# Two two-layer transformer blocks on one core: 32 of 48 modulation units as row sums on the vector engine instead of products on TensorE

## The chip, the cores and the metric

The kernel runs on one core of one Trainium2 chip. The metric is the time of one execution on the device in microseconds (us); lower is better. The kernel before takes 1193.03 us (median of three runs, 1192.88 to 1195.18).

## What is computed

Two blocks of two layers each follow one another on 256 tokens of width 1024, all in f32. The first block is attention of several kinds with a gate and a layer norm. The second has a stream of 256 latent tokens and one of 256 context tokens; its layer, cut to what matters here, is

```python
shift_x, scale_x, gate_x = split(silu(c)     @ w_mod + b_mod, 3)   # w_mod: 1024 x 3072
shift_c, scale_c, gate_c = split(silu(c_ctx) @ w_mod + b_mod, 3)
hx = rms_norm(xs, norm_g) * (1 + scale_x) + shift_x                # hc alike
px = hx @ w_in + b_in                                              # 1024 x 7712
ya, yb, yc = conv(px), gla(px), attention(px)                      # three branches
m  = (sigmoid(px[13])*ya + sigmoid(px[14])*yb + sigmoid(px[15])*yc) @ w_out
xs = xs + gate_x * m              # the context stream alike, in the first layer only
```

The **modulation** is the first two lines: two vectors (c and c_ctx) times a 1024 x 3072 matrix, once for each of the two layers. It depends on no token, so it may be computed at any time before its parts are used: shift and scale at the layer's norm, the gate at the layer's end.

## The kernel before

**Weights.** All weights are streamed from DRAM as units of 512 KB (128 partitions x 1024 f32) in one fixed table, by `WStream`. A unit is loaded by SP (L130) into one of `RAW` = 4 raw buffers `wr`; ACT casts it to a high part `wh` (L154); DVE subtracts to get the low part `wl` (L155); both have their own rings of buffers, 5 of `wh` and 5 + `WLX` = 5 of `wl`. The product then takes three matmuls, high by high, high by low and low by high (`mm3`, L184 to L186). `get(key)` is called as a unit's products are written; it first calls `ahead`, which issues the loads up to 6 table entries further on and the splits up to 3 (`LOOK`; 3 and 2 at the start). A scheduler sets the order of the instructions on each engine as the program is built; on the chip each engine works through its own in that order. Unit names in the trace: the first digit is the layer, `0m` the three kinds of merge gates of block two (8 units each), `0oa`, `0gg`, `0og`, `0cg`, `0oc` the branch gates and branch outputs between them, `0o` and `0p` the output product for the two streams, `0AKV`, `0AQ`, `0BQ` the attention's keys, values and queries, `0Va`, `0Vb` the convolution's inputs. Names with a capital letter A to I and `O` are those of block one.

**Modulation.** The 48 units of `w_mod` (2 layers x 3 parts x 8) are not split. They stand in the same table between the others, at the places of `FILL` (a key and a number), and each is taken by `mod_stream` just before the unit of that key: four f32 matmuls of 32 columns of `cz` (silu of c and c_ctx) by 128 x 256 of weights (L770), each recorded as two passes. After the 8 units of a part, ACT copies the sum out of PSUM (`modr`, L775), two small matmuls turn it (`modt`, L778) and DVE adds the bias (L782). The 24 units of layer 0 stand in the second layer of block one (keys 1A to 1H), 16 units of layer 1 in the first layer of block two, and 8 in its second layer.

**The first layer's merges** (about 545 to 820 us) are the longest stretch of one kind: for each of the three branches, eight 512-column merge-gate units and four branch-output units, interleaved, with the GLA branch and the convolution's taps (L1012, one multiply-add of 128 x 512 each) on DVE beside them.

Of the kernel before, what the change touches and what calls it, by code (L numbers as in the profile page):

```python
# [10 lines left out]
F32 = mybir.dt.float32  # L11
# [4 lines left out]
OP = mybir.AluOpType  # L16
# [16 lines left out]
NPA = (2, 3)  # L33
WLX = 0

# [75 lines left out]
class WStream:  # L111
# [118 lines left out]
def block1(g, l, xTh, xTl, xtok, W, last, pre_out=lambda: None, hold=None, each=None):  # L230
# [268 lines left out]
    def fox_gates():  # L499
# [23 lines left out]
        nc.tensor.matmul(ps[:, 128:256], lf[:, 1, :], g.tri, start=True, stop=False)  # L523
        nc.tensor.matmul(ps[:, 128:256], lf[:, 0, :], g.ones, start=False, stop=True)

# [207 lines left out]
def units_mod():  # L733
    return [(f'mod{s}{k}', k, 1, [(D * s, D)]) for s in MORDER for k in range(8)]

# [25 lines left out]

def mod_stream(g, l, W):

    nc, sp, pp = g.nc, g.sp, g.pp
    for s in MORDER:
        ps = pp.tile([128, 256], F32, name=f'mod{l}{s}', tag='gm', bufs=g.GM)
        for k in range(8):
            w = W.whole(f'{l}mod{s}{k}')
            for q in range(4):
                nc.tensor.matmul(ps[32 * q:32 * q + 32], g.cz[:, k // 2, 2 * (k % 2):2 * (k % 2) + 32],  # L770
                                 w[:, 0, 256 * q:256 * q + 256], start=k == 0, stop=k == 7)
            if k < 7:
                yield
        r = sp.tile([128, 256], F32, name=f'modr{l}{s}', tag='tg', bufs=TG)
        nc.scalar.copy(r, ps)  # L775
        pt = pp.tile([128, 2, 4, 2], F32, name=f'modt{l}{s}', tag='at', bufs=g.AT)
        for i in range(2):
            nc.tensor.matmul(pt[:, i].rearrange("p q w -> p (q w)"), r[:, 128 * i:128 * i + 128], g.sel8,  # L778
                             start=True, stop=True)
        ks = slice(8 * s, 8 * s + 8)  # L780
        v = lambda t: t.rearrange("p (q i) w -> p q i w", q=4)
        nc.vector.tensor_add(v(g.mod[l][:, ks, :]), pt.rearrange("p i q w -> p q i w"),  # L782
                             v(g.bmod[l][:, ks, None].to_broadcast([128, 8, 2])))
        if s == 1:

            nc.vector.scalar_tensor_tensor(g.modA[l], g.mod[l][:, ks, :], 1.0,
                                           g.ng[l][:, :, None].to_broadcast([128, 8, 2]), op0=OP.add, op1=OP.mult)
        yield
# [731 lines left out]
def host_arrays(inp):  # L1520
    h = dict(xa=pack_xa(xT_layout(inp['x'][0]), inp['w_in'][0]), xtok=inp['x'][0], ctxt=xT_layout(inp['ctx_2'][0]), cst=consts(CST),
             par1=par1(inp), par2=par2(inp), rowp=rowpar(inp), wup=wup(inp))
    for i, lst in enumerate(CST1):
        h[f'cst1{i}'] = consts(lst)
    for l in range(2):
# [3 lines left out]
        h[f'wm_{l}'] = pack(inp['w_mod_2'][l], units_mod())  # L1529
        h[f'wc_{l}'] = pack(inp['w_conv_out_2'][l], units_out('oc', 4))  # L1530
# [18 lines left out]
def setup(ctx, tc, ins):  # L1549
# [60 lines left out]
def setup_mod(g, ins, W):  # L1610
# [24 lines left out]
def setup2(g, ins):  # L1635
# [7 lines left out]
    for l in L:  # L1643
# [29 lines left out]

# [50 lines left out]
def program(ctx, tc, ins, out, parts=(1, 2)):  # L1724
    g = setup(ctx, tc, ins)
    nc = g.nc
    mods = sum((table(ins[f'wm_{l}'], f'{l}', units_mod()) for l in range(2)), [])
    f32 = {e[0] for e in mods}
    fs = FILL.split()
# [9 lines left out]
    for l in range(2):  # L1739
        t2 = tables2(ins, l)  # L1740
        o = [t2[f'{l}{k}'] for k in order2(l)]
        if l == 0:

            o = o[:7] + [(f'0BQ{i}', *e[1:]) for i, e in enumerate(o[3:7])] + o[7:]
            o += [(f'0p{i}', *e[1:]) for i, e in enumerate(o[-8:])]
        seq += o
    tab, m = [], 0
    for e in seq:
        n = fills.get(e[0], 0)
        tab += mods[m:m + n] + [e]  # L1750
        m += n
# [79 lines left out]
```

## Time and profile before

| | |
|---|---|
| median of three runs | 1193.03 us (1192.88 to 1195.18) |
| profiled execution | 1192.62 us, of which span of the trace 1190.8 us |
| granted TensorE clock | 0.999 |
| PE (TensorE) busy | 1168.5 us, 98% |
| DVE (VectorE) busy | 921.1 us, 77% |
| ACT (ScalarE) busy | 569.5 us, 48% |
| DMA moved | 171.33 MB, mean 144 GB/s |

The span is the traced part of the profiled execution; 1.8 us lie around it. Busy times count an instruction from its start to its end; instructions that follow each other closely on one engine overlap a little, so the distance from one start to the next is what an instruction costs there.

### The profile page before, as it was taken

To read this page: it belongs to the slowest core of one execution; us is meant where nothing else is said; L and a number is where in the kernel's file an instruction comes from. 1 tells how busy PE (TensorE), PEld (TensorE's weight loads), DVE (VectorE), ACT (ScalarE), POOL (GpSimd) and SP (SyncE) were. 2 spreads that over 40 slices of the span, in tenths; PEclk is the share of its full clock that TensorE was granted. 3 is DMA by queue.
4 is the path that set the end of the run, shared out by engine and by line. 5 is a ranking of instruction groups with operands and counts; after the bars stand their busy time and mean duration, and the time that the engine had idled before them with its cause. 6 is when DMAs were issued, how large, how long until landed. Compare 5 with 4: busy or idle time off the path is not lost.

```text
span 1190.8 us, 20632 instructions
## 1 busy us (share of the span) xinstructions
PE 1168.5 (98%) x8024; PEld 975.7 (82%) x8024; DVE 921.1 (77%) x2051; ACT 569.5 (48%) x1024; POOL 11.2 (1%) x42
## 2 busy tenths in 40 slices
PE   8999999999999999999999999999999999999998
PEld 6788777677887777767887888888999778999998
DVE  6996766967799859989545986755799897896984
ACT  5556634456555433247444422433455534855552
POOL 0000000000000000000000000000000000000000
PEclk9999999999999999999999999999999999999999
DMA  7634566465555642024221232325545333554552
GB/s 263 224 125 127 186 207 225 155 229 195 177 194 181 230 137 89 19 73 145 68 84 59 89 100 78 106 89 177 178 142 186 96 107 123 179 162 127 174 176 72
DMA packets 47538, 171.33 MB, mean 144 GB/s; under 512 B 5260, under 2 KB 5900, under 8 KB 46672
## 3 DMA queue, kind: packets, MB, share of 16 engines
q1 hardware_dynamic: 47440, 170.01, 43.7%
q8 instruction: 63, 1.03, 0.3%
q14 instruction: 35, 0.29, 0.1%
HBM read 167.89 MB, written 2.10 MB: 143 GB/s over the span
## 4 chain that ended last, share of the span: by engine, by line
PE 76%; DVE 11%; DMA 6%; ACT 5%; issue 2%; SPq 0%; ACTq 0%; DVEq 0%
PE f0m L186 3%; PE f0m L185 3%; PE f0m L184 3%; PE f1m L186 2%; PE f1m L184 2%; PE f1m L185 2%; PE po L185 1%; PE po L186 1%; PE po L184 1%; PE mod L770 1%; PE go L186 1%; PE go L185 1%; PE go L184 1%; PE yog L186 1%; PE yoc L186 1%
## 5 line engine op out<-in xcount | busy, mean ns | idle before, releaser
L1012 DVE SCALAR_TENSOR_TENSOR ucv<-up,par,ucv 128x512 f32<-128x512 f32 (+1 forms) x240 | 147.3, 614 | 2.8
L184 PE MATMUL f0m<-hTh,wh_0m 128*128 128x512 f32 x192 | 75.1, 391 | 0.0
L185 PE MATMUL f0m<-hTl,wh_0m 128*128 128x512 f32 x192 | 75.1, 391 | 0.0
L186 PE MATMUL f0m<-hTh,wl_0m 128*128 128x512 f32 x192 | 74.8, 390 | 0.0
L184 PE MATMUL f1m<-hTh,wh_1m 128*128 128x256 f32 x192 | 54.9, 286 | 0.1
L186 PE MATMUL f1m<-hTh,wl_1m 128*128 128x256 f32 x192 | 54.8, 286 | 0.0
L185 PE MATMUL f1m<-hTl,wh_1m 128*128 128x256 f32 x192 | 54.5, 284 | 0.0
L154 ACT CAST wh_0m<-wr_0m 128x1024 fp32r<-128x1024 f32 x24 | 25.1, 1047 | 55.9 <-PE f0m L185 14.5
L155 DVE TENSOR_TENSOR wl_0m<-wr_0m,wh_0m 128x1024 fp32r<-128x1024 f32 x24 | 29.3, 1222 | 18.2 <-ACT wh_0m L154 18.1
L184 PEld LDWEIGHTS f0m<-hTh,wh_0m 128*128 128x128 f32 x192 | 36.1, 188 | 7.4
L185 PEld LDWEIGHTS f0m<-hTl,wh_0m 128*128 128x128 f32 x192 | 36.1, 188 | 7.3
L186 PEld LDWEIGHTS f0m<-hTh,wl_0m 128*128 128x128 f32 x192 | 36.1, 188 | 7.3
L184 PEld LDWEIGHTS f1m<-hTh,wh_1m 128*128 128x128 f32 x192 | 36.8, 191 | 0.5 <-ACT wh_1m L154 0.3
L186 PEld LDWEIGHTS f1m<-hTh,wl_1m 128*128 128x128 f32 x192 | 36.7, 191 | 0.2 <-DVE wl_1m L155 0.2
L185 PEld LDWEIGHTS f1m<-hTl,wh_1m 128*128 128x128 f32 x192 | 36.8, 191 | 0.1
L154 ACT CAST wh_1m<-wr_1m 128x1024 fp32r<-128x1024 f32 x24 | 24.9, 1049 | 24.4 <-PE f1m L185 7.6
L155 DVE TENSOR_TENSOR wl_1m<-wr_1m,wh_1m 128x1024 fp32r<-128x1024 f32 x24 | 29.3, 1221 | 8.6 <-ACT wh_1m L154 8.4
L155 DVE TENSOR_TENSOR wl_0o<-wr_0o,wh_0o 128x1024 fp32r<-128x1024 f32 x8 | 9.8, 1224 | 13.2 <-ACT wh_0o L154 13.2
L1413 DVE SCALAR_TENSOR_TENSOR xT<-po,mod,xT 128x256 f32<-128x256 f32 x16 | 7.7, 483 | 14.3 <-PE po L186 14.3
L185 PE MATMUL po<-mgl,wh_0o 128*128 128x256 f32 x64 | 18.2, 285 | 0.0
L186 PE MATMUL pp<-mgh,wl_0p 128*128 128x256 f32 x64 | 18.2, 284 | 0.0
L185 PE MATMUL pp<-mgl,wh_0p 128*128 128x256 f32 x64 | 18.2, 284 | 0.0
(1857 smaller groups left out, 3960.6 us busy)
## 6 DMA issues: line engine op xcount, KB each, us to landing
wr_0mod<-in_wm_dram SPq DMA_DIRECT2D x24, 512.0 KB, 4.5
wr_1mod<-in_wm_dram SPq DMA_DIRECT2D x24, 512.0 KB, 3.7
wr_0m<-in_w_dram SPq DMA_DIRECT2D x24, 512.0 KB, 3.5
wr_1m<-in_w_dram SPq DMA_DIRECT2D x24, 512.0 KB, 3.5
wr_0O<-in_w1o_dram SPq DMA_DIRECT2D x8, 512.0 KB, 3.6
wr_1O<-in_w1o_dram SPq DMA_DIRECT2D x8, 512.0 KB, 3.6
wr_0o<-in_wo_dram SPq DMA_DIRECT2D x8, 512.0 KB, 3.6
wr_0p<-in_wo_dram SPq DMA_DIRECT2D x8, 512.0 KB, 3.7
```

The source lines that it names most:

```text
L154: g.nc.scalar.copy(wh, r)
L155: g.nc.vector.tensor_sub(wl, r, wh.bitcast(F32))
L184: nc.tensor.matmul(out, lh, rh, start=start, stop=False)
L185: nc.tensor.matmul(out, lh, rl, start=False, stop=False)
L186: nc.tensor.matmul(out, ll, rh, start=False, stop=stop)
L770: nc.tensor.matmul(ps[32 * q:32 * q + 32], g.cz[:, k // 2, 2 * (k % 2):2 * (k % 2) + 32], w[:, 0, 256 * q:256 * q + 256], start=k == 0, st ...
L1012: yield nc.vector.scalar_tensor_tensor(o, src, dw[:, i, j:j + 1], o, op0=OP.mult, op1=OP.add)
L1413: nc.vector.scalar_tensor_tensor(r[:, f, :], ps[:, :256], g.mod[l][:, 16 + f, w:w + 1], r[:, f, :], op0=OP.mult, op1=OP.add)
```

## The change

16 units (layer 0, parts 1 and 0) stay as products, at the first seven of the old places, in the second layer of block one. The other 32 units (layer 0 part 2, and all three parts of layer 1) are laid out transposed: a unit holds 256 output columns of `w_mod` on 128 partitions by two, and half (512) of the inner dimension along the row. For each unit DVE does four SCALAR_TENSOR_TENSOR instructions of 128 x 512 that multiply by a broadcast row of silu(c) or silu(c_ctx) (`modc`) and sum along the row with `accum_out`; the product itself goes to a scratch tile `modj` in bf16 that nobody reads. The two halves are added later. The 32 units are spread evenly over the 48 units from `0m3_1` to `0oc3`, the first layer's merges (`DFILL`). `modc` (512 KB, the same 4 KB row on every partition) is loaded by SP twice, once per half, and takes two tanh on ACT and two instructions on DVE each time.

The tiles for this are paid with three others: `wl` has 4 buffers instead of 5 (`WLX`), the table of ones has one column, and the rope table of block two, until now a constant, is loaded by SP twice, once for each layer. `ahead` now counts only split units, so that modulation units in the table no longer shorten the look-ahead.

```diff
-WLX = 0
+WLX = -1
-MORDER = (1, 0, 2)
-FILL = '1B2 2 1E2 3 1D2 3 1F0 2 1G0 2 1H2 1 0Va0 2 0Va1 2 0Va2 2 0GV0 1 0ag0 2 0ag2 2 1GV0 3 1ag0 2 1ag2 2 1A0 1 0BQ2 2 1F2 2 1GK0 1 1B0 1 1A3 5 1C2 1 0ag1 1 1H0 1 0GK0 2'
+FILL = '1A0 1 1A3 5 1B0 1 1B2 2 1E2 3 1C2 1 1D2 3'
+DFILL = ((32, '0m3_1', '0oc3'),)
+LATE = 1
+MODP = [(0, 1), (0, 0)]
+MODD = [(*m, c, h) for ms, hs in (([], (0, 1)), ([(0, 2), (1, 1), (1, 0), (1, 2)], (1, 0)))
+        for h in hs for m in ms for c in range(4)]
...
     def whole(self, key):
         i = self.idx[key]
-        self.ahead(i)
+        while self.nd <= i:
+            self._dma()
...
+    def behind(self, i, n):
+        while n and i < len(self.table) - 1:
+            i += 1
+            n -= self.table[i][0] not in self.f32
+        return i
+
     def ahead(self, i):
-        while self.nd < min(len(self.table), i + self.ad + 1):
+        while self.nd < min(len(self.table), self.behind(i, self.ad) + 1):
             self._dma()
-        while self.ns < min(len(self.table), i + self.asp + 1):
+        while self.ns < min(len(self.table), self.behind(i, self.asp) + 1):
...
         self.ahead(i)
+        for _ in range(self.dots.pop(key, 0)):
+            next(self.dotstream)
         return self.spl[i]
...
+def mod_dots(g, W):
+    nc, sp = g.nc, g.sp
+    junk = g.cp.tile([128, 512], BF, name='modj')
+    have, seen = None, set()
+    for l, s, c, h in MODD:
+        if h != have:
+            cb, have = sp.tile([128, 2, 512], F32, name=f'modc{l}{s}{h}', tag='modc', bufs=1), h
+            nc.sync.dma_start(cb, g.csrc[1024 * h:1024 * h + 1024][None, :].to_broadcast([128, 1024])
+                              .rearrange("p (w k) -> p w k", w=2))
+            for w in range(2):
+                t = g.t2([128, 512], f'modt{l}{s}{h}{w}')
+                nc.scalar.activation(t, cb[:, w], AF.Tanh, scale=0.5)
+                nc.vector.scalar_tensor_tensor(cb[:, w], t, 1.0, cb[:, w], op0=OP.add, op1=OP.mult)
+        x = W.whole(f'{l}mod{s}{c}{h}')
...
+        for b in range(2):
+            for w in range(2):
+                nc.vector.scalar_tensor_tensor(junk, x[:, b], 0.5, cb[:, w], op0=OP.mult, op1=OP.mult,
+                                               accum_out=half[:, 2 * c + b, w:w + 1])
...
-CST = [('ident', 128), ('ones', 128), ('rope2', 256), ('gmask', 256), ('sel8', 8), ('hm', 4), ('zc', 2)]
+CST = [('ident', 128), ('ones', 1), ('gmask', 256), ('sel8', 8), ('hm', 4), ('zc', 2)]
...
+    rc = g.t2([128, 2, 2, 64], f'rope2c{l}')
+    nc.sync.dma_start(rc, g.rope2src.rearrange("p (a t d) -> p a t d", a=2, t=2))
...
+        for i in range(n):
+            k = a + i * (b - a) // n
+            at.setdefault(keys[k + LATE], []).append(dots[m])
+            use[keys[k]] = use.get(keys[k], 0) + 1
```

The order of the instructions shows three places. The first is SP's queue at the start of the program, before the change:

```order
L1691 DMA xa_86<-in_xa_dram 128x716
L1691 DMA xa_94<-in_xa_dram 128x716
L1691 DMA xa_102<-in_xa_dram 128x1432
L1691 DMA xa_110<-in_xa_dram 128x1432
L1691 DMA xa_118<-in_xa_dram 128x1432
L1583 DMA cst_126<-in_cst_dram 128x256
```

and after it:

```order
L1761 DMA xa_86<-in_xa_dram 128x716
L829 DMA modc_5714<-in_ccr_dram 128x1024
L1761 DMA xa_94<-in_xa_dram 128x716
L1761 DMA xa_102<-in_xa_dram 128x1432
L1761 DMA xa_110<-in_xa_dram 128x1432
L1761 DMA xa_118<-in_xa_dram 128x1432
```

The first load of `modc`, which is needed only in the merges, is now the second entry, ahead of four of the five `xa` loads that bring the first weights and the input.

The second place is DVE around the second `0AQ` unit in the first layer of block two, with the semaphores that each instruction waits for; before:

```order
L208 SCALAR_TENSOR_TENSOR ln10y<-ln10t,ln10y 128x1
L194 TENSOR_SCALAR ln11v<-lss_3600 128x1 [waits Activation_49]
L155 TENSOR_TENSOR wl_0AQ_3804<-wr_0AQ_3525,wh_0AQ_3803 128x1024 [waits DMAHW4_49]
L201 SCALAR_TENSOR_TENSOR ln10t<-ln10y,ln10h 128x1 [waits DVE_49]
L195 TENSOR_SCALAR ln11y<-ln11v 128x1 [waits DVE_49]
L196 TENSOR_SCALAR ln11h<-ln11v 128x1
L210 SCALAR_TENSOR_TENSOR ln10t<-ln10t 128x1 [waits DVE_49]
```

after:

```order
L208 TENSOR_SCALAR xn0v<-s_3367 128x1 [waits Activation_49]
L159 TENSOR_TENSOR wl_0AQ_3751<-wr_0AQ_3470,wh_0AQ_3750 128x1024 [waits DMAHW5_49,PE_49]
L209 TENSOR_SCALAR xn0y<-xn0v 128x1 [waits DVE_49]
L208 TENSOR_SCALAR xn1v<-s_3368 128x1 [waits Activation_49]
L210 TENSOR_SCALAR xn0h<-xn0v 128x1
L209 TENSOR_SCALAR xn1y<-xn1v 128x1 [waits DVE_49]
L210 TENSOR_SCALAR xn1h<-xn1v 128x1
```

The split of `0AQ` (`wl_0AQ`) gained a wait for PE, since its buffer is now one that the products of four units earlier still read. In the whole program 92 of 256 splits wait for PE before the change and 162 after it.

The third place is DVE in the first layer's merges, at the last units of the first branch (`wl_0m_6`, `wl_0m_7`, `wl_0oa`); before:

```order
L155 TENSOR_TENSOR wl_0oa_5997<-wr_0oa_5894,wh_0oa_5996 128x1024
L155 TENSOR_TENSOR wl_0m_6_6031<-wr_0m_6_5928,wh_0m_6_6030 128x1024
L1312 SCALAR_TENSOR_TENSOR acc_0_5630<-mtm_0_5959,yoa_6000 128x512
L1312 SCALAR_TENSOR_TENSOR acc_0_5630<-mtm_0_5992,yoa_6014 128x512
L155 TENSOR_TENSOR wl_0m_7_6064<-wr_0m_7_5961,wh_0m_7_6063 128x1024
L155 TENSOR_TENSOR wl_0oa_6097<-wr_0oa_5994,wh_0oa_6096 128x1024
L155 TENSOR_TENSOR wl_0gg_6131<-wr_0gg_6028,wh_0gg_6130 128x1024
L1312 SCALAR_TENSOR_TENSOR acc_0_5631<-mtm_0_6059,yoa_6100 128x512
```

after:

```order
L159 TENSOR_TENSOR wl_0m_6_5910<-wr_0m_6_5793,wh_0m_6_5909 128x1024
L842 SCALAR_TENSOR_TENSOR modj,mod_1340<-wr_1mod_5830,modc_5714 128x512 x3
L842 SCALAR_TENSOR_TENSOR modj,mod_1340<-wr_1mod_5865,modc_5714 128x512 x3
L159 TENSOR_TENSOR wl_0m_7_5947<-wr_0m_7_5832,wh_0m_7_5946 128x1024
L842 SCALAR_TENSOR_TENSOR modj,mod_1340<-wr_1mod_5865,modc_5714 128x512
L842 SCALAR_TENSOR_TENSOR modj,mod_1340<-wr_1mod_5905,modc_5714 128x512 x4
L159 TENSOR_TENSOR wl_0oa_5986<-wr_0oa_5867,wh_0oa_5985 128x1024
L842 SCALAR_TENSOR_TENSOR modj,mod_1340<-wr_1mod_5981,modc_5714 128x512
L1375 SCALAR_TENSOR_TENSOR acc_0_5511<-mtm_0_5942,yoa_5989 128x512
```

Where two or three splits followed one another, each has now one to two units of dots (`modj,mod_...`) between it and the next. The dots on other places of the merges stand alike among the GLA branch's steps and the taps.

## Rows read from the trace of the kernel before

**Rows 1.** The page: the span, and busy time of each engine.
```profile
span 1190.8 us, 20632 instructions
...
PE 1168.5 (98%) x8024; PEld 975.7 (82%) x8024; DVE 921.1 (77%) x2051; ACT 569.5 (48%) x1024; POOL 11.2 (1%) x42
```

**Rows 2.** The page: the chain that ended last, by engine.
```profile
PE 76%; DVE 11%; DMA 6%; ACT 5%; issue 2%; SPq 0%; ACTq 0%; DVEq 0%
```

**Rows 3.** Busy us by stage: from:to, length, PE, PEld, DVE, ACT, POOL; clock; DMA share; GB/s.
```profile
240.00:300.00 60.00, 55.36 (x449) 43.28 (x451) 40.19 (x93) 37.23 (x104) 0.17 (x2) 1.00 0.59 200
345.00:410.00 65.00, 63.23 (x368) 49.51 (x368) 61.85 (x240) 35.61 (x66) 0.00 (x0) 1.00 0.57 195
...
545.00:820.00 275.00, 273.21 (x1581) 225.42 (x1577) 183.07 (x315) 113.29 (x180) 0.62 (x8) 1.00 0.29 89
...
660.00:712.00 52.00, 52.00 (x231) 43.09 (x230) 49.19 (x67) 18.59 (x24) 0.00 (x0) 1.00 0.30 92
712.00:740.00 28.00, 28.00 (x132) 23.31 (x131) 14.81 (x22) 7.00 (x8) 0.17 (x2) 1.00 0.30 94
740.00:770.00 30.00, 29.91 (x142) 24.37 (x141) 27.07 (x70) 13.39 (x18) 0.46 (x6) 1.00 0.30 88
```

**Rows 4.** PE in order of time around one unit in block one (start, duration).
```profile
164.22 0.37 PE L185 MATMUL g1A<-wl_1A,xTh 128*128 128x460 f32 x1
164.52 0.64 PE L770 MATMUL mod<-wr_0mod,cz 128*32 128x256 f32 x8
165.09 0.48 PE L186 MATMUL g1A<-wh_1A,xTl 128*128 128x460 f32 x1
```

**Rows 5.** PE in order of time around two units in block two.
```profile
373.52 0.40 PE L186 MATMUL t0BQ<-wh_0BQ,hTl 128*128 128x512 f32 x1
373.85 1.07 PE L770 MATMUL mod<-wr_1mod,cz 128*32 128x256 f32 x16
374.85 0.73 PE L184 MATMUL t0BQ<-wh_0BQ,hTh 128*128 128x512 f32 x2
```

**Rows 6.** The small matmuls that end a part (duration min/median/max).
```profile
L778 PE MATMUL modt<-cst,modr x24: 171/256/277, 189.0 to 1007.1; 128*128 128x8 f32 x24
```

**Rows 7.** PE and DVE in order of time around two units at 0Va0.
```profile
381.86 1.07 PE L770 MATMUL mod<-wr_1mod,cz 128*32 128x256 f32 x16
...
382.06 1.22 DVE L155 TENSOR_TENSOR wl_0BQ<-wr_0BQ,wh_0BQ 128x1024 fp32r<-128x1024 f32 x1
...
383.43 0.40 PE L185 MATMUL t0BQ<-wl_0BQ,hTh 128*128 128x512 f32 x1
```

**Rows 8.** DVE in order of time: multiply and sum along rows, 128 x 512.
```profile
150.38 0.68 DVE L669 SCALAR_TENSOR_TENSOR mx<-xtok,go 128x512 f32<-128x512 f32 x1
...
150.99 0.68 DVE L669 SCALAR_TENSOR_TENSOR mx<-xtok,go 128x512 f32<-128x512 f32 x1
```

**Rows 9.** DVE in order of time: multiply and sum along rows, 128 x 64.
```profile
79.45 0.22 DVE L431 SCALAR_TENSOR_TENSOR lscr<-par 128x64 f32<-128x64 f32 x1
```

**Rows 10.** DVE in order of time: the split of a unit in the merges.
```profile
694.56 1.22 DVE L155 TENSOR_TENSOR wl_0og<-wr_0og,wh_0og 128x1024 fp32r<-128x1024 f32 x1
```

**Rows 11.** PE in order of time: the first use of that unit's low part.
```profile
715.05 0.39 PE L185 MATMUL yog<-ygg,wh_0og 128*128 128x512 f32 x1
715.28 0.39 PE L186 MATMUL yog<-ygg,wl_0og 128*128 128x512 f32 x1
```

**Rows 12.** ACT and PE in order of time at the start of the program.
```profile
3.56 0.40 ACT L1697 CAST xTh<-xa 128x256 fp32r<-128x256 f32 x1 [1.54 <-DMA xa<-in_xa_dram]
...
5.03 0.41 ACT L1697 CAST xTh<-xa 128x256 fp32r<-128x256 f32 x1 [0.59 <-DMA xa<-in_xa_dram]
...
8.49 0.62 ACT L1697 CAST xTh<-xa 128x512 fp32r<-128x512 f32 x1 [2.58 <-DMA xa<-in_xa_dram]
...
10.02 0.69 PE L184 MATMUL g0A<-wh_0A,xTh 128*128 128x460 f32 x2 [2.00 <-ACT wh_0A L154]
...
10.31 0.62 ACT L1697 CAST xTh<-xa 128x512 fp32r<-128x512 f32 x1 [0.34 <-DMA xa<-in_xa_dram]
```

More of the change, by code (lines that the diff above doesn't have):

```diff
@@ L1 @@
-import itertools
 import math
@@ L523, in fox_gates @@
         nc.tensor.matmul(ps[:, 128:256], lf[:, 1, :], g.tri, start=True, stop=False)
-        nc.tensor.matmul(ps[:, 128:256], lf[:, 0, :], g.ones, start=False, stop=True)
+        nc.tensor.matmul(ps[:, 128:256], lf[:, 0, :], g.ones.to_broadcast([128, 128]), start=False, stop=True)
         nck = sc['c'] = sp.tile([128, 256], F32R, name=f'nck{l}', tag='tg', bufs=TG)
@@ L733, in units_mod, with pack_mod @@
 def units_mod():
-    return [(f'mod{s}{k}', k, 1, [(D * s, D)]) for s in MORDER for k in range(8)]
+    return [(f'mod{s}{k}', k, 1, [(D * s, D)]) for _, s in MODP for k in range(8)]
+def pack_mod(l, w):
+    wt = w.T.reshape(24, 128, 2, 512)
+    parts = [pack(w, units_mod())] if l == 0 else []
+    for ll, s, c, h in MODD:
+        if ll == l:
+            f = 8 * s + 2 * c
+            parts.append(wt[f:f + 2, :, h].transpose(1, 0, 2).reshape(-1))
+    return np.concatenate(parts)
 def _seq(n, k):
@@ L759, with mod_mm @@
 TAPG = ((0, 0, 6, 4), (3, 3, 14, 10))
-def mod_stream(g, l, W):
+def mod_mm(g, W):
     nc, sp, pp = g.nc, g.sp, g.pp
-    for s in MORDER:
+    for l, s in MODP:
         ps = pp.tile([128, 256], F32, name=f'mod{l}{s}', tag='gm', bufs=g.GM)
@@ L784, in mod_stream, with mod_gain @@
         if s == 1:
-            nc.vector.scalar_tensor_tensor(g.modA[l], g.mod[l][:, ks, :], 1.0,
-                                           g.ng[l][:, :, None].to_broadcast([128, 8, 2]), op0=OP.add, op1=OP.mult)
+            mod_gain(g, l)
+        yield
+def mod_gain(g, l):
+    g.nc.vector.scalar_tensor_tensor(g.modA[l], g.mod[l][:, 8:16, :], 1.0, g.ng[l][:, :, None].to_broadcast([128, 8, 2]),
+                                     op0=OP.add, op1=OP.mult)
+def mod_dots(g, W):
[12 more added lines that the diff above has]
+        x = W.whole(f'{l}mod{s}{c}{h}')
+        m = g.mod[l][:, 8 * s:8 * s + 8, :]
+        second = (l, s, h ^ 1) in seen
+        if c == 0:
+            half = sp.tile([128, 8, 2], F32, name=f'modh{l}{s}', tag='modh', bufs=2) if second else m
+        for b in range(2):
+            for w in range(2):
+                nc.vector.scalar_tensor_tensor(junk, x[:, b], 0.5, cb[:, w], op0=OP.mult, op1=OP.mult,
+                                               accum_out=half[:, 2 * c + b, w:w + 1])
+        if c == 3:
+            seen.add((l, s, h))
+            if second:
+                nc.vector.tensor_add(m, m, half)
+                nc.vector.tensor_add(m, m, g.bmod[l][:, 8 * s:8 * s + 8, None].to_broadcast([128, 8, 2]))
+                if s == 1:
+                    mod_gain(g, l)
         yield
@@ L1455, in consts @@
     hm = np.stack([i % 4 == h for h in range(4)], 1)
-    d = dict(hm=hm, zc=np.stack([((i >= 64) & (i < 96)) | (i == 97), (i == 97) * 1.0 - (i == 96)], 1), ident=np.eye(128), tri=le, ones=np.ones((128, 128)), cmul=le.T, clow=np.where(le.T, 0, LOW),
-             causal=np.where(le.T, 0, NEG), rope1=rope_tab1(), hsel=hs.reshape(128, 512), rope2=rope_tab2(),
-             gmask=gm, sel8=np.stack([(i // 32 == c // 2) & ((i % 32 == c % 2) | (i % 32 == 30 + c % 2)) for c in range(8)], 1))
+    d = dict(hm=hm, zc=np.stack([((i >= 64) & (i < 96)) | (i == 97), (i == 97) * 1.0 - (i == 96)], 1), ident=np.eye(128), tri=le, ones=np.ones((128, 1)), cmul=le.T, clow=np.where(le.T, 0, LOW),
+             causal=np.where(le.T, 0, NEG), rope1=rope_tab1(), hsel=hs.reshape(128, 512),
+             gmask=gm,
+             sel8=np.stack([(i // 32 == c // 2) & ((i % 32 == c % 2) | (i % 32 == 30 + c % 2)) for c in range(8)], 1))
     return np.concatenate([d[n].astype(np.float32) for n, _ in lst], axis=1)
@@ L1524, in host_arrays @@
         h[f'cst1{i}'] = consts(lst)
+    h['rope2'] = rope_tab2()
+    h['ccr'] = np.ascontiguousarray(np.stack([inp['c_ctx_2'].reshape(2, 512), inp['c_2'][0].reshape(2, 512)], axis=1)).reshape(-1)
     for l in range(2):
@@ L1654, in setup2 @@
     g.rowsrc = {}
+    g.rope2src = ins['rope2']
     rp = ins['rowp']
@@ L1726, in program @@
     nc = g.nc
-    mods = sum((table(ins[f'wm_{l}'], f'{l}', units_mod()) for l in range(2)), [])
-    f32 = {e[0] for e in mods}
+    mods = table(ins['wm_0'], '0', units_mod())
+    dots, at = [], [len(mods) * 128 * 1024, 0]
+    for l, s, c, h in MODD:
+        dots.append((f'{l}mod{s}{c}{h}', ins[f'wm_{l}'], at[l], 2, 512))
+        at[l] += 128 * 1024
+    f32 = {e[0] for e in mods + dots}
     fs = FILL.split()
@@ L1746, in program @@
         seq += o
+    keys = [e[0] for e in seq]
+    use, at, m = {}, {}, 0
+    for n, a, b in DFILL:
+        a, b = keys.index(a), keys.index(b) + 1
+        for i in range(n):
+            k = a + i * (b - a) // n
+            at.setdefault(keys[k + LATE], []).append(dots[m])
+            use[keys[k]] = use.get(keys[k], 0) + 1
+            m += 1
+    assert m == len(dots)
     tab, m = [], 0
@@ L1749, in program @@
         n = fills.get(e[0], 0)
-        tab += mods[m:m + n] + [e]
+        tab += mods[m:m + n] + at.get(e[0], []) + [e]
         m += n
@@ L1755, in program @@
     W = WStream(g, tab, looks, f32, fills)
-    W.stream = itertools.chain(mod_stream(g, 0, W), mod_stream(g, 1, W))
+    W.stream, W.dots, W.dotstream = mod_mm(g, W), use, mod_dots(g, W)
     xsp = g.dram.tile([128, 2048], F32, name='xsp')
```

8 lines of the change are left out of this document (4 added, 4 removed).

## The prediction

> **What bounds the kernel now.** I read the page's busy times first: PE is busy for 1168.5 of 1190.8 us, DVE for 921.1 [rows 1]. The chain of waits says the same in another way: 76% of it is PE, 11% DVE, 6% DMA [rows 2]. So time taken from PE counts nearly in full, and time given to DVE counts only where DVE is already late. Where that is, the table by stage tells [rows 3]. At 345 to 410 us DVE is busy for 61.85 of 65 us: this stage belongs to DVE. At 240 to 300 us neither is full (PE 55.36 of 60) and the DMA engines are at 0.59: PE waits there for weights. In the first layer's merges, 545 to 820 us, PE is full (273.21 of 275) and DVE has 92 us to spare, but unevenly: 49.19 of 52 us at 660 to 712, 27.07 of 30 at 740 to 770, 14.81 of 28 between them. The change moves work from the full engine to the one with room; the question is whether the room is where the work goes.
>
> The sum is made against the profiled execution, 1192.62 us (a span of 1190.8 and 1.8 around it); the median of the runs is 0.4 us higher.
>
> **What PE gets back.** One modulation unit costs PE what it pushes the next product apart. Around a single unit the products start at 164.22 and 165.09, 0.87 us apart; a normal step of 512 columns is 0.23 [rows 11], so 0.21 for 460 columns, and the unit costs 0.66 [rows 4]. Around two units it is 373.52 to 374.85, 1.33 us less 0.23, or 1.10, so 0.55 each [rows 5]. The places that lose their units:
> - Block one, second layer: three pairs and two singles, 3 x 1.10 + 2 x 0.66 = 4.6 us.
> - 0BQ2 and 0Va0 to 0Va2: four pairs, 4.4 us, but in the stage that belongs to DVE. There the pair at 381.86 stands beside a DVE split that runs from 382.06 to 383.28, and the product that waits for it starts at 383.43 [rows 7]: without the pair PE would have waited for that split all the same. I count half, 2.2 us (bounds 0 and 4.4).
> - 0GK0 to 0ag2: three pairs, two singles, 4.6 us, with PE full.
> - Second layer of block two: a single, two pairs and a triple (at 0.55 each), 4.5 us.
> - Four of six part ends go, each with two small matmuls of 0.26 us [rows 6]. At the ratio of step to duration of the neighbours, 0.23 to 0.39 [rows 11], eight of them take 8 x 0.26 x 0.58 = 1.2 us (bounds 0 and their durations, 2.1).
>
> Together 17.1 us, with bounds of 13.7 (the pairs in DVE's stage and the part ends at nothing) and 20.2. It can be more in one place: block one's eight removed units are also eight loads of 512 KB less in the stretch where PE idles 4.6 us at 0.59 DMA share [rows 3]; if those loads were what it waited for, up to 4.6 us more come back.
>
> **What the dots cost.** 32 units of four instructions are 128 sums along rows of 128 x 512. The trace has the instruction: two of them start 0.61 us apart, readout included [rows 8]. So 128 x 0.61 = 78 us, and with the four that make `modc` (about the same each) 80.5 us. The stretch then holds 183.1 + 80.5 = 263.6 of 275 us of DVE work, 96%. That is hidden as long as the splits stay ahead of PE. In the trace a split ends at 695.78 (694.56 + 1.22) [rows 10] and PE first uses it at 715.28 [rows 11]: 19.5 us ahead. A merge unit is 24 steps of 0.23, 5.5 us, and with one `wl` buffer less a split can start one unit later, so the lead is 14.0 us. Spread evenly, the dots put 15.2 us into the 52 us from 660 to 712, which makes 64.4 of 52: 12.4 us of the lead are eaten. The next stretch gives back 5.0 (14.81 + 8.2 of 28), the one at 740 to 770 takes 5.9 (27.07 + 8.8 of 30). The lead falls to about 1 us and doesn't end. But DVE doesn't only split: what it takes from PSUM comes late by as much, and in DVE's own stage its busy share was 95%, not 100 [rows 3]; 263.6 / 0.95 is 277.5, 2.5 us over. I take 3.5 us, 2.5 and one for the dips, with bounds of 0 and, at a usable share of 0.85, 310 - 275 - 14 = 21 us.
>
> [...]
>
> **What one `wl` buffer less costs.** Splits that wait for PE rise from 92 to 162 of 256. In the merges that is the shorter lead, counted above. Where the lead is 0 already, as at 383.28 to 383.43 [rows 7], a split that must wait for a buffer makes PE wait in its turn, and behind the waiting split on DVE stand the norm's and the attention's small steps. The three 0AKV buffers stay in use beside 0AQ, so one of four is left for 0AQ, where two were: at worst each of the four 0AQ units and a few of the second layer's waits its whole split, 7 x 1.2 = 8 us. At best nothing, since DVE order and not the ring decides there now. It may even give a little back, because the raw buffers there no longer hold modulation units. I take 1.5, nearer to nothing because no product before shows a wait on that ring.
>
> **The start.** `modc` is now second in SP's queue. The input's parts of 716 KB arrive 1.82 us apart (8.49, 10.31) and PE waits 2.00 us for one of them at 10.02 [rows 12], so nothing covers 512 KB put ahead of them: 1.82 x 512 / 716 = 1.3 us. Bounds: 0, if the queues had room while loads were still being issued, and 2.1 by the slower pace of the first two parts (358 KB in 1.47 us, 3.56 to 5.03). The two rope loads of 131 KB are 0.3 us of transfer each by that pace, issued before their use; nothing, or 0.6 if late. ACT's four tanh, each on 128 x 512, fall in a stretch where ACT is busy 113.29 of 275 us [rows 3]: nothing. The second `modc` load waits for the sixteenth unit's dots, and the seventeenth's wait for it, 1.3 us of transfer and two tanh; that is in the dips above.
>
> Sum: -17.1 + 1.3 + 1.5 + 3.5 = -10.8 us, 1181.8 on the profiled execution and **1182.2** on the median's scale.
>
> **Rivals.**
> - *DVE becomes the bound in the merges* (the slower side). Dots stand in order ahead of splits and of what empties PSUM; each is only 0.61 us, but DVE has 4% left. Nothing is gained once the merges lose 14.3 us: 275 + 14 + 14.3 = 303.3, that is a usable share under 263.6 / 303.3 = 0.87. At 0.85 the time is 1182.2 + 21 - 3.5 = 1199.7. For it: the local sums above end within 1 us of the lead. Against: 0.95 at 345 to 410, where DVE's chains are worse. Chance 0.14.
> - [...] Chance 0.04.
> - *Everything comes back*: 20.2 us, 4.6 more in block one, the start and the buffers at 1 together, the merges at nothing: 1193 - 23.8 = 1169. For it: DVE's 92 idle us. Chance 0.15 for 1168 to 1176.
> - *The units were filler.* If in DVE's stage and in block one PE only waits where it multiplied (13.7 - 4.6 = 9.1 left), and the ring costs 4: 1193 - 9.1 + 1.3 + 4 + 3.5 = 1192.7, no change; halfway to the forecast 1187.5. Chance 0.22 for 1187 to 1195, of which half is within the bound.
>
> **How the numbers follow.** The forecast, 1176 to 1187, has 0.45. No change is within 0.2%, 2.4 us, about what a measurement of this kernel can tell: 1190.6 to 1195.4. Faster: 0.45 + 0.15 + 0.11 = 0.71. Same 0.11. Slower 0.18, from the first two rivals. The range leaves out the slow tail of the first rival and the second, and the deep end of the third: 1170 to 1197.
>
> **What would show it.** PE's busy time falls by about 17 us, and no matmul of the modulation is left after the D units of block one's second layer. [...] The first `xTh` cast after 8.49 comes 1.3 us later. In 545 to 820 DVE is at 95% or more with PE still above 98%; PE waits for `wl_0m`, `wl_0og` or `wl_0oc` in sum of some 3 us there. More than 14 us of such waits is the first rival. At 345 to 410 PE waits for `wl_0AQ` for at most 2 us; 8 would make the forecast wrong by 6.

## The result, and the profile after

The kernel after takes 1174.17 us (median of four runs, 1171.35 to 1174.94), beside 1192.95 for the kernel before (four runs too): ratio 0.9843, 95% interval 0.9822 to 0.9863. Forecast were 1182.2 and a range of 1170 to 1197. It became faster, as forecast, by 18.8 us instead of 10.8. That is outside the forecast's own 1176 to 1187 and inside 1168 to 1176, the third rival's, which had a chance of 0.15. The profiled execution took 1173.71 us.

The page of the kernel after, where it answers to [rows 1, 2]:

```profile
span 1171.9 us, 20383 instructions
...
PE 1146.5 (98%) x7752; PEld 968.5 (83%) x7752; DVE 996.6 (85%) x2315; ACT 571.1 (49%) x1024; POOL 11.2 (1%) x42
...
PE 72%; DVE 15%; DMA 5%; ACT 5%; issue 3%; SPq 0%; ACTq 0%; DVEq 0%
```

PE is as full as before, with 22 us less to do (about 17 were forecast). DVE is busy for 75.5 us more; its share of the chain of waits is 4 points larger, PE's 4 points smaller. By stage, with the columns of [rows 3]:

```profile
240.00:300.00 60.00, 58.61 (x454) 48.63 (x453) 43.97 (x103) 39.40 (x110) 0.55 (x6) 1.00 0.42 136
345.00:410.00 65.00, 60.82 (x300) 49.26 (x300) 59.40 (x218) 37.20 (x67) 0.00 (x0) 1.00 0.46 147
545.00:820.00 275.00, 271.63 (x1555) 224.97 (x1554) 255.17 (x570) 108.31 (x171) 2.62 (x12) 1.00 0.49 156
640.00:700.00 60.00, 59.90 (x269) 49.47 (x268) 59.31 (x106) 21.28 (x29) 0.00 (x0) 1.00 0.40 122
700.00:730.00 30.00, 28.41 (x134) 23.43 (x133) 28.68 (x81) 7.22 (x8) 0.17 (x2) 1.00 0.58 175
```

At 240 to 300 us PE's idle time fell from 4.6 to 1.4 us, as DMA's share fell from 0.59 to 0.42. In the merges DVE is at 93% (255.17 of 275; 95% or more were forecast), and at 99% at 640 to 700, while PE stays full there.

The stages don't stand at the same microseconds in the two traces, so the time is best followed from one first product to another. The table has the microseconds between the first products of the units named, in each profiled execution; the two middle columns belong to experiments below (32 units left out; their loads alone kept).

| from - to | before | units out | loads kept | after |
|---|---|---|---|---|
| start - 1B | 181.6 (1.7) | 180.6 | 180.7 | 180.6 |
| 1B - 1I | 125.1 | 116.3 | 124.5 (3.4) | 118.8 |
| 1I - 0AKV | 35.7 | 35.8 | 35.8 | 35.9 |
| 0AKV - 0GK | 92.7 | 87.3 | 89.7 | 89.4 |
| 0GK - 0m | 118.6 | 111.2 | 113.4 | 111.1 |
| 0m - 1AQ (the merges, 0o, 0p) | 321.6 | 322.5 | 321.8 | 324.7 |
| 1AQ - 1gg | 184.0 | 178.7 | 183.5 (1.7) | 179.7 |
| 1gg - end | 127.7 | 127.7 | 127.7 | 127.8 |

In brackets is what stands in the stage for a lower granted clock: 2 us at 0.50, for instance, are counted as one us lost. That count is an estimate; in the trace of before, products of 460 columns start 0.38 us apart at 12 to 14 us, at a clock of 0.50, and 0.21 us apart at 16 to 18 us, at 1.00. The clock differs from one execution of a kernel to the next (over the whole span 0.994 to 1.000 in e9; last section), so it has to be taken out first. The start of the profile of before holds such a fall:

```profile
8.00:10.00 2.00, 0.02 (x1) 0.00 (x0) 0.69 (x1) 1.48 (x2) 0.00 (x0) 1.00 1.01 414
10.00:12.00 2.00, 1.52 (x4) 1.08 (x5) 1.90 (x3) 1.48 (x2) 0.00 (x0) 0.81 1.03 408
12.00:14.00 2.00, 2.00 (x7) 1.69 (x7) 1.90 (x3) 1.48 (x2) 0.00 (x0) 0.50 1.03 414
14.00:16.00 2.00, 2.00 (x10) 1.81 (x9) 1.32 (x3) 1.05 (x1) 0.00 (x0) 0.84 1.02 410
```

The clock column reads 0.81, 0.50 and 0.84: (0.19 + 0.50 + 0.16) x 2 = 1.7 us. The kernel after shows 1.00 there. Without it the two profiles differ by 17.3 us, not 19.0.

### The profile page after: what moved, and what is told of

It reads as the page before. It is cut to its first block, busy times and chain, and to the rows that moved or that the text cites. A ratio compares the mean times of both kernels' runs of the same rounds, so it can differ in the third digit from the quotient of the medians.

```text
span 1171.9 us, 20383 instructions
## 1 busy us (share of the span) xinstructions
PE 1146.5 (98%) x7752; PEld 968.5 (83%) x7752; DVE 996.6 (85%) x2315; ACT 571.1 (49%) x1024; POOL 11.2 (1%) x42
## 4 chain that ended last, share of the span: by engine, by line
PE 72%; DVE 15%; DMA 5%; ACT 5%; issue 3%; SPq 0%; ACTq 0%; DVEq 0%
PE f0m L200 2%; PE f0m L198 2%; PE f0m L199 2%; PE f1m L200 2%; PE f1m L198 2%; PE f1m L199 2%; DVE modj L842 2%; PE po L198 1%; PE po L199 1%; PE po L200 1%; DVE ucv L1075 1%; PE go L199 1%; PE go L198 1%; PE go L200 1%; PE yoc L200 1%
## 5 line engine op out<-in xcount | busy, mean ns | idle before, releaser
L200 PE MATMUL f0m<-hTh,wl_0m 128*128 128x512 f32 x192 | 75.5, 393 | 0.0
L842 DVE SCALAR_TENSOR_TENSOR modj<-wr_1mod,modc 128x512 bf16<-128x512 f32 x96 | 65.9, 687 | 9.1 <-DMA wr_1mod<-in_wm_dram 8.1
L158 ACT CAST wh_0m<-wr_0m 128x1024 fp32r<-128x1024 f32 x24 | 25.2, 1051 | 53.1 <-DMA wr_0m<-in_w_dram 42.9
L1362 ACT ACTIVATE mtm<-f0m,hbin 128x512 f32<-128x512 f32 x24 | 16.4, 685 | 19.0 <-PE f0m L200 16.7
L842 DVE SCALAR_TENSOR_TENSOR modj<-wr_0mod,modc 128x512 bf16<-128x512 f32 x32 | 22.0, 686 | 0.5
L198 PE MATMUL pp<-mgh,wh_0p 128*128 128x256 f32 x64 | 18.3, 285 | 0.0
```

The source lines that it names most:

```text
L158: g.nc.scalar.copy(wh, r)
L198: nc.tensor.matmul(out, lh, rh, start=start, stop=False)
L200: nc.tensor.matmul(out, ll, rh, start=False, stop=stop)
L842: nc.vector.scalar_tensor_tensor(junk, x[:, b], 0.5, cb[:, w], op0=OP.mult, op1=OP.mult, accum_out=half[:, 2 * c + b, w:w + 1])
L1362: nc.scalar.activation(sg, pm, AF.Tanh, scale=0.5, bias=hb[:, blk(n, f)])
```

## The experiments

All ratios are to the kernel before on the same chip, with 95% intervals. Executions of one kernel spread by several us (seventeen of the kernel before, measured beside e9, from 1189.56 to 1197.80), so a difference under about 2 us is read from the traces, with the granted clock taken out, or not at all. A trace is one execution too: from 1B to 1I the instructions of PE, DVE and ACT stand in the same order in five profiles (after, e1, e5, e6, e11), and without clock they take 117.2 to 119.8 us there.

**Where modc is loaded (e1, e2).** The first run puts the load of `modc` back behind the inputs, the second puts a useless one in front of them in the kernel before.

```diff
...
+            if not seen:
+                g.after(d, W.loads['0GK0'])       # e1, in the kernel after
...
+        if j == 0:                                # e2, in the kernel before
+            dm = g.sp.tile([128, 1024], F32, name='dum', tag='wraw', bufs=g.RAW)
+            W.last = nc.sync.dma_start(dm, ins['rowp'][0:1024][None, :].to_broadcast([128, 1024]))
...
```

> The kernel after the change, with the first load of modc put behind the load of 0GK0 instead of second in SP's queue; nothing else. Theory A (spacing): the early load cost nothing, because with it the five input parts arrive evenly and PE never waits 2 us for one, so that its products in the first 20 us keep the step of 0.21 us instead of 0.38. Then this kernel shows the 2 us wait and the 0.38 steps of before again, and is 0.5 to 1.5 us slower than the kernel after (its 1174.2), ratio to before 0.985. Theory B (transfer): 512 KB ahead of the inputs delay them by 1.3 us and something else paid for it; then this kernel is about 1.3 us faster than the kernel after, 1172.9, and the last product of 0A starts earlier than 19.1 us.

> The kernel before with one useless 512 KB load (a 4 KB row on all partitions, never read) second in SP's queue; nothing else. Theory A (spacing): the wait of 2.00 us at 10.0 us goes, the steps stay at 0.21, and the time falls by 0.3 to 1.0 us to about 1192.3 although more is loaded. Theory B (transfer): the inputs come 1.3 us later and the time rises by 1.3 to about 1194.3.

Measured: e1 1175.56 us, 0.9842 (0.9822 to 0.9861), the same as the kernel after; e2 1193.03 us, 0.9995 (0.9981 to 1.0009), the same as before. By time nothing is told apart. e1's trace looks as theory A said: uneven inputs, a wait of PE of 1.52 us, and a clock of 0.50 at 12 to 14 us. Two other traces contradict the theory. In e2 the inputs arrive as evenly as in the kernel after (casts at 7.52, 9.32, 11.13 and 12.98 us), yet PE waited 1.72 us and the clock fell to 0.50 at 12 to 14 us. And the run without the 32 units (e3, below), whose start is that of before, with uneven inputs, waited only 0.94 us and kept its clock. So the early load makes the inputs arrive evenly, but that doesn't decide whether the clock falls. In profiles where it doesn't fall there, 0B's first product comes at 18.14 to 18.43 us without the early load (e3, e4 and e7, with four raw buffers as in the kernel after) and at 18.90 to 19.57 with it (the kernel after, e6, e8, e11, e12): it costs 0.5 to 1.4 us, which agrees with the 1.3 of the forecast.

**The units left out, with five and with four wl buffers (e3, e4).** In the kernel before:

```diff
-FILL = '1B2 2 1E2 3 1D2 3 1F0 2 ...'
+FILL = '1A0 1 1A3 5 1B0 1 1B2 2 1E2 3 1C2 1 1D2 3'
...
-    mods = sum((table(ins[f'wm_{l}'], f'{l}', units_mod()) for l in range(2)), [])
+    mods = table(ins['wm_0'], '0', units_mod())[:16]
...
-WLX = 0
+WLX = -1                                          # e4 only
```

> The kernel before without the 32 units (matmuls, loads, part ends) that the change moves; five wl buffers, no dots, no early modc, old tables. Leaves out: the modulation of layer 0 part 2 and of all of layer 1, which are set to constants. Theory A (PE's time and the waits around the units): the units cost 20 to 23 us, more than the 17.1 forecast, since they also held raw buffers and split attention steps; time 1170 to 1173. Theory B (the forecast's prices): 17.1 us, time 1175.9, and what the kernel after gained beyond it comes from its other edits.

> As the run without the 32 units, with four wl buffers instead of five; the same is left out. The forecast took 1.5 us for the lost buffer, bounds 0 and 8. Theory A: in the ledger by unit the kernel after loses 0.7 us at 1AQ and little else where no dots stand, so 0.5 to 1.5 us slower than with five. Theory B: the buffer costs several us in the attention stage at 345 to 410 and was paid there out of the pairs' gain: 3 to 8 us slower than with five.

Measured: e3 1166.21 us, 0.9777 (0.9755 to 0.9798); e4 1169.40 us, 0.9793 (0.9774 to 0.9811). The units were worth 28 us by the medians (24 to 29 by the interval), and 25.2 by the profiles (26.9 us between the last products, less the 1.7 of clock): more than theory A's 20 to 23, far more than the 17.1 of the forecast. Four buffers cost 3.5 us against five by the profiles, of which 1.7 is a fall of the clock at 375 to 379 us; the rest, 1.8, is a little over theory A's 0.5 to 1.5 and the forecast's 1.5. It lies at 0AKV to 0GK (1.2) and 1AQ to 1gg (1.4), with 0.9 less in the merges.

**The dots (e5, e6).** In the kernel after, left out, and half of them done twice:

```diff
-                nc.vector.scalar_tensor_tensor(junk, x[:, b], 0.5, cb[:, w], ...)
+                pass                              # e5; the 32 loads go too
...
+                for _ in range(2 - w):            # e6
+                    nc.vector.scalar_tensor_tensor(junk, x[:, b], 0.5, cb[:, w], ...)
```

> The kernel after without its dots: the 128 sums and the loads of the 32 transposed units are left out (their part of the modulation is set to constants); modc, the four wl buffers and the new tables stay. Theory A (the ledger by unit): in the merges the kernel after loses 2.9 us where no product was added, by DVE coming late; without dots it is 3 us faster than the kernel after, about 1171, and at 0gg to 0cg no product waits for DVE. Theory B: that loss is not the dots' but the wl ring's; then the time stays within 1 us of 1174. If the dots cost much more than the ledger shows, 1168 or less.

> The kernel after with 192 sums instead of 128: those with the first of the two rows are done twice, into the same place; nothing else. That is 64 x 0.61 to 0.73 = 39 to 47 us more on DVE in the merges. Theory A (the lead is the reserve): the lead of the splits falls from 15 to 3.3 us already, and DVE stands idle for 20 of 275 us; so PE pays 15 to 35 us, time 1189 to 1209. Theory B (DVE still has room, since only 2.9 us are lost now): under 6 us slower, 1180 or less.

Measured: e5 1172.15 us, 0.9835 (0.9813 to 0.9858); e6 1202.49 us, 1.0090 (1.0075 to 1.0105), slower than the kernel before. From 0m to 1AQ, e5 takes 321.5 us, the kernel after 324.7 and e6 352.5, of which 5.1 are clock. So 128 dots with their 32 loads cost 3.2 us and 64 more cost 23: theory A in both, for e5 by its trace alone, since its time isn't told apart from the kernel after's. In the kernel after one split of the third branch ends at 777.13 us and its product starts at 780.41:

```profile
775.90 1.23 DVE L159 TENSOR_TENSOR wl_0m<-wr_0m,wh_0m 128x1024 fp32r<-128x1024 f32 x1
```
```profile
780.41 0.39 PE L200 MATMUL f0m<-hTh,wl_0m 128*128 128x512 f32 x1
```

These rows are DVE's and PE's in order of time; they answer to [rows 10, 11], where the distance was 19.5 us. 3.3 us is the least of all units in the merges; it was 15 at 650 us, as worked out (14.0), and from there falls. In e6 it is at most 0.1 us at 15 of the last 21 merge units, and PE's longest waits from 0m to 1AQ read:

```profile
PE yog L198 <- ACT wh_0og L158: 4.1, 2, 3.6
PE f0m L198 <- ACT wh_0m L158: 3.4, 3, 1.9
PE f0m L200 <- DVE wl_0m L159: 3.0, 5, 0.9
```

(us in total, times, longest). That is the first rival, reached with half as many dots again.

**The loads of the units by themselves (e7, e9, e10).** In the kernel before, the 32 units are still loaded and taken at their places, but by one matmul of 32 columns; e10 has five raw and four wl buffers besides, e9 has these in the full kernel before.

```diff
-            for q in range(4):
+            for q in range(4 if full else 1):
+                n = 256 if full else 32
...
-KN = (5, 3, 4, 5, 2, 12, 6, 5, 2, 4)
+KN = (5, 3, 5, 5, 2, 12, 6, 5, 2, 4)              # e9, e10: RAW = 5, and WLX = -1
```

> The kernel before with the 32 units still loaded and taken at their places, but with one matmul of 32 columns each instead of four of 256, and without part ends (the modulation they carry is set to constants). Against the run without the units (1166.2) it shows what their loads alone cost. Theory A (the raw ring): with four raw buffers a unit keeps the next weights from being loaded, so splits come late where their lead is near 0; 5 to 8 us and 32 x 0.1 to 0.15 us for the small matmuls: 1174 to 1179, with DVE's waits for wh_1F to wh_1I as in before. Theory B (PE's time alone): 1169 to 1171, without those waits.

> The kernel before with five raw buffers and four wl buffers instead of four and five; full computation, all 48 units as products. Theory A (the raw ring): the 32 units cost about 6 us over PE's own time because each keeps one of four raw buffers from the next weights; a fifth gives most of that back, less the 1.7 us of the wl buffer: 1187 to 1190. Theory B (the loads cost by their transfer time, or the order of the products): a fifth buffer gives nothing, 1194 to 1196.

> As the run in which the 32 units are only loaded and taken by one small matmul each (1178.9; the modulation they carry is left out), with five raw and four wl buffers. Theory A (the raw ring): 4 to 6 us back, 1.7 lost: 1174.5 to 1176.6, and SP's waits for mod at 215 to 310 and 370 to 450 us shrink. Theory B: 1180 to 1181.

Measured: e7 1178.89 us, 0.9897 (0.9882 to 0.9912), 12.7 above e3 (14 by the ratios). By the profiles it is 16.8, less 5.1 of clock, 11.7. The small matmuls explain about 5: two of them (four records) take 0.31 us in the trace of e7, so 32 x 0.16 by estimate. The other 6.7 us are what the units cost without PE's work. Where, the waits of DVE for ACT's cast at 228 to 310 us tell (us in total, times, longest); before:

```profile
DVE wl_1F L155 <- ACT wh_1F L154: 6.2, 2, 4.4
DVE wl_1G L155 <- ACT wh_1G L154: 3.7, 1, 3.7
DVE wl_1H L155 <- ACT wh_1H L154: 3.4, 3, 1.7
DVE wl_1I L155 <- ACT wh_1I L154: 2.6, 3, 1.4
```

with the loads alone:

```profile
DVE wl_1F L155 <- ACT wh_1F L154: 5.4, 2, 3.7
DVE wl_1H L155 <- ACT wh_1H L154: 2.8, 2, 1.7
DVE wl_1G L155 <- ACT wh_1G L154: 2.4, 1, 2.4
DVE wl_1I L155 <- ACT wh_1I L154: 1.2, 1, 1.2
```

and without the units:

```profile
DVE wl_1I L155 <- ACT wh_1I L154: 1.0, 1, 1.0
```

So the splits of the neighbouring weights came late because of the units' presence in the stream, not of their matmuls. The trace of before shows one way, at the longest of these waits (PE, SP's queue, ACT and DVE in order of time):

```profile
249.72 1.07 PE L770 MATMUL mod<-wr_0mod,cz 128*32 128x256 f32 x16
250.85 0.37 SPq L130 DMA_DIRECT2D wr_1F<-in_w_dram  x1
256.38 1.05 ACT L154 CAST wh_1F<-wr_1F 128x1024 fp32r<-128x1024 f32 x1 [1.01 <-DMA wr_1F<-in_w_dram]
257.46 1.23 DVE L155 TENSOR_TENSOR wl_1F<-wr_1F,wh_1F 128x1024 fp32r<-128x1024 f32 x1 [4.41 <-ACT wh_1F L154]
```

The load of 1F is issued as the products of the pair before it end and free a raw buffer; the cast waits for its landing, the split for the cast, and behind the split on DVE stand steps of the attention. PE's longest waits in this stage are for the attention's steps on DVE and ACT, not for weights (before, 240 to 300 us):

```profile
PE dft L477 <- DVE dfe L473: 1.9, 2, 1.6
PE fo10po L389 <- ACT fo10T L381: 1.2, 1, 1.2
PE dft L477 <- DVE dn10y L211: 0.8, 1, 0.8
```

How much of the 6.7 us the raw ring makes isn't settled. With a fifth raw buffer, e10 takes 1178.40 us, 0.9875 (0.9854 to 0.9896), and e9 1194.70, 1.0011 (0.9991 to 1.0031): theory B by the time of e9, neither in e10. By the profiles, less the clock, e10 is 3.1 us shorter than e7, which would be theory A, but 1.8 of them lie before 1B, where none of the 32 units stand; e9 is 0.6 us longer than before. The four kinds of waits above shrink, from 15.9 us in before to 5.6 in e9 and from 11.8 in e7 to 8.3 in e10, but 1B to 1I is only 1.8 and 1.3 us shorter for it, and 0AKV to 0GK isn't shorter (91.0 us in e10, 89.7 in e7). The sign that theory A named failed: SP's waits for the units' products (`mod`) at 215 to 310 and 370 to 450 us are 23.9 and 14.0 us in e7, and 29.2 and 15.6 in e10. A third cause fits as well: in the kernel before the units count in the look-ahead of three table entries, so that three units in a row leave no split ahead; the change ended that too. It was not tried by itself. With the 16 units that stay, 1B to 1I is no shorter under the new rule (117.2 to 119.8 us in the five profiles named above) than under the old (116.3 in e3 and e4).

**Versions with more or other dots (e8, e11, e12).** Eight more units as dots in block one (e8); the dots of the merges moved off the taps (e11); both (e12).

```diff
-DFILL = ((32, '0m3_1', '0oc3'),)
+DFILL = ((8, '1B3', '1H2'), (32, '0m3_1', '0oc3'))                        # e8
+DFILL = ((18, '0m3_1', '0m2_1'), (14, '0m1_2', '0o3'))                    # e11
+DFILL = ((8, '1B3', '1H2'), (18, '0m3_1', '0m2_1'), (14, '0m1_2', '0o3')) # e12
...
```

> The kernel after with eight of the 16 remaining products (layer 0 part 0) as dots too, spread from 1B3 to 1H2 in block one, and modc loaded once more; the full computation. PE gets back 8 x 0.55 to 0.66 = 4.4 to 5.3 us. Theory A (DVE has room there, 43.97 of 60 us busy at 240 to 300): 32 x 0.67 = 21 us of dots are hidden but for 1 us; time about 1170. Theory B (order and ring decide there, the leads of the splits are 0 to 3 us, and dots stand ahead of softmax steps): 1174 to 1180.

> The kernel after with its dots moved off the densest stretch: 18 units between 0m3_1 and 0m2_1, 14 between 0m1_2 and 0o3, none while the taps and the convolution's norm run; every second sum writes its product into the unit itself instead of the scratch tile. Full computation. Theory A (the lead is the reserve): the waits for DVE in the merges (2 to 3 us, and the one of 1.6 us at 728) go: 1171 to 1172.5. Theory B: the dots are late wherever they stand, since the merges' last units and the output units have leads of 9 us only: 1174 or more.

> As the run before it, with the eight units of layer 0 part 0 as dots in block one too (the run with those alone gave 1173.2, with more of its execution at a lower granted clock than the kernel after's). Full computation. Theory A: both gains add, 1167.5 to 1171. Theory B: the dots in block one bring waits of PE there, after some of which the clock falls, which takes the gain back: 1173 or more.

Measured: e8 1173.22 us, 0.9843 (0.9829 to 0.9858); e11 1176.66, 0.9876 (0.9846 to 0.9905); e12 1177.04, 0.9859 (0.9835 to 0.9882). None beats the kernel after by its time. Moving the dots won nothing, as theory B said, but not for its reason: in e11 the lead of the splits is never under 9.0 us, and 14 to 15 at the last units of the merges, and 0m to 1AQ still takes 324.8 us. The wait of 1.6 us at the taps went and another came, for a small step of the GLA branch behind dots:

```profile
PE gl010cum L1217 <- DVE la L1210: 1.7, 1, 1.7
```

In e8's profile falls of the clock cost 8.5 us, 6.8 of them in block one, one beside a wait of PE of 3.25 us; without them e8 would end 4.2 us before the kernel after, and e12, alike, 2.7. That fits the theory that waits in block one take the gain back. It isn't one execution's chance: the clock over the whole span is 0.992 to 0.996 in e8's five executions and 0.993 to 0.997 in e12's, and 0.998 to 1.000 in four of the kernel after. That the waits are the cause of these falls isn't shown.

## Why the prediction was right in direction and short in size

- **What PE gets back** was mis-sized: 17.1 us counted, 25.2 found (e3). Stage by stage, without clock: 8.8 us from 1B to 1I where 4.6 were counted; 5.4 from 0AKV to 0GK where 2.2 were; 7.4 from 0GK to 0m against 4.6; 5.3 in the second layer against 4.5; the 1.2 of the part ends is in these, and 1.6 are lost elsewhere. Two things failed in it. The pairs at 0BQ2 to 0Va2 were not hidden behind DVE: nothing of their 4.4 us was. The split in [rows 7] was one that PE would have waited for; without the units that split itself comes earlier: it ends 40.9 us after the stage's first product in before, 31.7 in e3, and again 40.9 in e7, where the loads are kept. And a unit's price was read from PE's steps alone [rows 4, 5], which see its matmuls (25.2 - 6.7 = 18.5 us, near the 17.1 + 2.2 that full pairs give) but not the 6.7 us that its presence in the stream cost by late splits. That was in the text only as 4.6 us that "can be more in one place", in the third rival, and with PE waiting for weights; PE waited for steps of the attention (above). The measured time is that rival's, but not its sum, which put the merges at nothing.
- **The dots**: 3.5 us forecast, 3.2 measured (e5). The lead of the splits is a reserve, as said, and its shape was nearly right: 15 us at 650, falling with the taps, 3.3 at the least, where 1 was worked out. e6 spends it. But it is not what the 3.2 us were paid from, so the agreement of the sums is in part luck: the forecast took 1 us for the dips of the lead and 2.5 from a usable share of 0.95, which no run tested. PE waited not for `wl_0m`, `wl_0og` or `wl_0oc` but for small steps of other work that stood behind dots and had no lead:

```profile
PE cvt L1400 <- DVE cv01t L215: 1.6, 1, 1.6
PE gl010cum L1217 <- DVE la L1210: 0.8, 1, 0.8
PE gn00t L1326 <- DVE gw L1323: 0.4, 1, 0.4
```

  These are all but two of PE's waits at 535 to 830 us in the kernel after.
- **One wl buffer less**: 1.5 forecast, 1.8 measured (e4). The 8 us bound was not approached.
- **The start**: 1.3 forecast, 0.5 to 1.4 measured at 0B's first product. The forecast's sign that it would be seen, casts about 1 us later, was there (the last at 13.15 after 12.13 us). That the kernel after is 1.0 us ahead at 1B all the same (180.6, before 181.6) is luck: the profile of before lost 1.7 us there to its clock, and this one nothing.
- **The second rival** had 0.04 for sums much slower than those of [rows 8]; no run shows that. In the kernel after a dot takes 0.66 to 0.70 us; one that follows another directly starts 0.72 to 0.74 us after it, where 0.61 was forecast, and most other instructions start 0.61 or 0.62 us after a dot (last section).
- Not explained: less the clock, the kernel after's profile is 6.2 us longer than that of e4 (32 units out, four `wl` buffers). 3.1 of them are the merges, but 2.4 lie from 1B to 1I (118.8 and 116.3 us), where no dots stand. That can be scatter in part: one wait of PE there, for the same instruction, is 2.19 us in the kernel after, 0.86 in e5 and 2.64 in e1, which all have the same order. But all five profiles of that order are above 116.3. What differs there is the rule of the look-ahead, which was not tried by itself.

## What to carry to other kernels

When work is taken off a full engine, its price is not only its steps on that engine (here about 18.5 of 25.2 us): ask what its operands held while they waited (here a raw buffer and a place in the look-ahead) and read the waits of the neighbours that came after. When work is put on an engine that feeds the full one, the reserve is not its idle share but the distance between what it feeds and the use; add up work stretch by stretch against that distance, and test it by adding half as much again (here 128 dots cost 3.2 us and 64 more 23). Small steps without such a distance can be late while the reserve is unspent, as here and in e11; look for them by themselves. A unit's removal and its stand-in (the loads without the product) are two cheap runs that tell the parts of a gain apart.

## What the runs showed of the hardware

- After some waits of PE the granted clock fell to 0.50 for a while, after others not. At about 10 us it fell after a wait of 2.00 us in the kernel before and one of 1.52 in e1, and not after one of 0.94 in e3. At the same place, at about 220 us, PE waiting for the same instruction, the kernel after waited 2.19 us and e1 2.64, and both stayed at 1.00; e2 waited 2.19 and e7 2.33, and both fell. In e7 the stretch reads:

```profile
218.00:220.00 2.00, 1.38 (x4) 1.08 (x4) 1.90 (x6) 2.00 (x5) 0.00 (x0) 0.69 0.51 197
220.00:222.00 2.00, 2.00 (x6) 1.18 (x5) 2.00 (x7) 1.08 (x2) 0.00 (x0) 0.50 0.82 209
222.00:224.00 2.00, 2.00 (x9) 1.16 (x11) 2.00 (x9) 0.00 (x0) 0.00 (x0) 0.50 0.73 172
224.00:226.00 2.00, 2.00 (x12) 1.02 (x8) 2.00 (x10) 0.00 (x0) 0.00 (x0) 0.61 0.46 154
```

  (0.31 + 0.50 + 0.50 + 0.39) x 2 = 3.4 us lost in one fall; others cost 1.7, as in the profile of before, or 5.1 (e9). The fourteen profiles have between none and four such falls ahead of the last products, and what decides isn't shown. In e9 they make much of the difference between executions: of its twelve the longest, 1199.0 us, had a clock of 0.994 over the whole span, the shortest, 1188.4, one of 1.000; by that difference of 0.006, an estimate, they are about 7 of the 10.6 us between them.
- In the kernel after every dot writes `modj`. Where a dot follows another directly and waits for nothing (41 times), it starts 0.72 to 0.74 us after it; where another instruction does (78 times), that starts 0.61 or 0.62 us after it in 68 cases and 0.59 to 0.81 in the rest (DVE in order of time):

```profile
629.08 0.68 DVE L842 SCALAR_TENSOR_TENSOR modj<-wr_1mod,modc 128x512 bf16<-128x512 f32 x1
629.69 0.08 DVE L842 DVE_READ_ACCUMULATOR modj<-wr_1mod,modc 128x1 f32 x1
629.81 0.69 DVE L842 SCALAR_TENSOR_TENSOR modj<-wr_1mod,modc 128x512 bf16<-128x512 f32 x1
```

  In e11 every second sum writes into the half unit that it and the one before it read. In these rows that one starts 0.73 us after the sum before it, and the next, which writes `modj`, 0.62 us after it; what makes the difference isn't shown:

```profile
599.12 0.69 DVE L842 SCALAR_TENSOR_TENSOR wr_1mod<-wr_1mod,modc 128x512 f32<-128x512 f32 x1
599.74 0.08 DVE L842 DVE_READ_ACCUMULATOR wr_1mod<-wr_1mod,modc 128x1 f32 x1
599.74 0.69 DVE L842 SCALAR_TENSOR_TENSOR modj<-wr_1mod,modc 128x512 bf16<-128x512 f32 x1
600.35 0.08 DVE L842 DVE_READ_ACCUMULATOR modj<-wr_1mod,modc 128x1 f32 x1
600.47 0.69 DVE L842 SCALAR_TENSOR_TENSOR wr_1mod<-wr_1mod,modc 128x512 f32<-128x512 f32 x1
```
